# The attention's rotary score products over 128 partitions instead of 64

## The chip, the cores and the metric

The kernel runs on one core of one Trainium2 chip. The metric is the time of one execution on the device in microseconds; lower is better. The engines are called TensorE (PE, with PEld for its weight loads), VectorE (DVE), ScalarE (ACT), GpSimd (POOL) and SyncE (SP), which issues the loads.

## The reference

One residual block of a streaming encoder over 256 tokens of width 2048, all in float32. After an RMS norm, two branches run side by side, retention with 8 heads and a multi-head latent attention with 16 heads; their outputs are gated by sigmoids, added and projected, and a squared-ReLU MLP of width 8192 follows. The part that the change touches is the scores of the latent attention. A head's query and key have 128 plain elements and 64 rotary ones, and the rotary key is the same for all heads:

```python
q_nope, q_pe = q[..., :QK_NOPE], _rope(q[..., QK_NOPE:], positions)
kv = (_rmsnorm(c_kv, kv_a_norm_g) @ w_kv_b).reshape(B, S, MLA_HEADS, QK_NOPE + V_HEAD)
k_nope, v = kv[..., :QK_NOPE], kv[..., QK_NOPE:]
k_pe = _rope(k_pe.reshape(B, S, 1, QK_ROPE), positions)
qf = jnp.concatenate([q_nope, q_pe], axis=-1)
kf = jnp.concatenate([k_nope, jnp.broadcast_to(k_pe, (B, S, MLA_HEADS, QK_ROPE))], axis=-1)
my = _block_causal_attention(qf, kf, v, MLA_QK_DIM ** -0.5)
```

The mask lets a token see its own chunk of 64 tokens and all earlier ones, so the first 128 queries see only the first 128 keys.

## The kernel before

Activations lie transposed, features on the partitions. Nearly all matrix products keep float32 accuracy by splitting each operand into a rounded part (`hi`, type float32r, cast on ScalarE) and the remainder (`lo`, subtracted on VectorE), and adding three products: hi with hi, hi with lo, lo with hi. `weights` does this for a weight tile (L168 the cast, L169 the subtraction), `split` for an activation (L550, L551), `mm3` issues the three products (L583 to L585). Where a product isn't split, as for the first 128 queries' scores, it is a plain float32 product.

The stages follow each other: the first projections, retention, its output, the latent vectors (`cc`), the gates (`gm`), the attention, its output projection (`mo`), the gates' merge, the output projection (`wo`), and the MLP (`zs`, `z`, `dn`). In the stage of the gates and in the MLP the order of the instructions is written out by hand; in the attention a scheduler sets it at build time, each engine's stream being fixed from then on.

The attention goes in four groups of four heads. `mla_projections(g)` makes the queries, keys and values of a group from `cc` (products `lt`, L199 and L201; values `v`, L214 to L217). `join` adds the two halves of such a product (L540, L541). The rotary queries of a group are two tiles `pe` of 128 partitions, each with one head in partitions 0 to 63 and one in 64 to 127; `rope` turns them, and their last 128 queries are split into `pes`, which lies in the big tile `vkp`. The rotary key `kpe` is there twice, in partitions 0 to 63 and in 64 to 127, and its split `kps` lies in `vkp` too. While a group's projections run, `mla_attention` runs the group before: `mla_scores` (tile `ms`), the softmax on VectorE (L1018, L1021, L1027) and ScalarE (L1023, L1029), `mla_turn`, which transposes the probabilities (`mt`, L1036), and `mla_values` (`my`; L583 to L585 and L1052). The last group runs beside the first columns of `mo`.

In `mla_scores`, the first 128 queries take two float32 products (L1010 plain, L1011 rotary); the other 128 queries take three products of rounded parts with the plain key and three with the rotary key, each of 256 columns. The four rotary ones take the 64 partitions of their head.

Of the kernel before, what the change touches and what calls it, by code (L numbers as in the profile page):

```python
# [12 lines left out]
F32 = mybir.dt.float32  # L13
# [4 lines left out]
ALU = mybir.AluOpType  # L18

P = 128  # L20
# [85 lines left out]
def block_kernel(ctx: ExitStack, tc: tile.TileContext, A):  # L106
    nc = tc.nc
    V, SC, G, PE = nc.vector, nc.scalar, nc.gpsimd, nc.tensor
# [7 lines left out]
    def big(name, dt=F32, shape=(P, KT, S)):  # L116
        return act.tile(list(shape), dt, tag="act16", name=name)
# [31 lines left out]
    def mmps(name):  # L149
        return pmm.tile([P, 512], F32, tag="mm", name=name)  # L150

    def atps(name):
        return pat.tile([P, 512], F32, tag="at", name=name)
# [3 lines left out]
    def wtile(kind, shape):  # L157
        uid[0] += 1
        dt, bufs = (F32, 5) if kind == "raw" else (F32R, 4)
        return wp.tile(shape, dt, tag=kind, bufs=bufs, name=f"{kind}{uid[0]}")  # L160
# [33 lines left out]
    def lora_pair(src, x, spare=False):  # L194
        hi, lo = weights(src, [P, 2, LT, P])
        for i in range(2):
            ps = (atps if spare and i else mmps)(f"lt{uid[0]}{i}")
            for k in range(LT):
                PE.matmul(ps, hi[:, i, k], x.both(k), start=k == 0, stop=False)  # L199
            for k in range(LT):  # L200
                PE.matmul(ps[:, :S], lo[:, i, k], x.hi(k), start=False, stop=k == LT - 1)  # L201
            yield i, ps

    def n_unit(outs, src, x, k0, nk, start, stop):
        for kh in range(0, nk, 2):
            w = weights(src[:, kh : kh + 2], [P, 2, 512])
            first, last = start and kh == 0, stop and kh == nk - 2
            for t, out in enumerate(outs):
                n_tile(out, w, x, t, k0 + kh, 2, first, last)
# [328 lines left out]
    def join(out, ps):  # L538
        t = rope_pool.tile([P, S], F32, tag="join", bufs=2, name="join")
        SC.copy(t, ps[:, S:])  # L540
        V.tensor_tensor(out=out, in0=ps[:, :S], in1=t, op=ALU.add)  # L541
# [6 lines left out]
    def split(hi, lo, val, scale=None):  # L548
        if scale is None:
            SC.copy(hi, val)  # L550
            V.tensor_tensor(out=lo, in0=val, in1=hi.bitcast(F32), op=ALU.subtract)  # L551
        else:
            SC.activation(hi, val, AF.Copy, scale=scale)
            V.scalar_tensor_tensor(
                lo, in0=val, scalar=scale, in1=hi.bitcast(F32), op0=ALU.mult, op1=ALU.subtract
            )
# [24 lines left out]
    def mm3(out, st, mv, start=True, stop=True):  # L581
        (sh, sl), (mh, ml) = st, mv
        PE.matmul(out, sh, mh, start=start, stop=False)  # L583
        PE.matmul(out, sh, ml, start=False, stop=False)
        PE.matmul(out, sl, mh, start=False, stop=stop)  # L585
# [15 lines left out]
    for k in range(KT):  # L601
        t = lead0[:, N_VEC:] if k == 0 else wtile("raw", [P, LEAD])
# [82 lines left out]
    def rope(out, ps, cos, sin, step):  # L685
        n = ps.shape[1]
        tmp = rope_pool.tile([P, n, S], F32, tag="rope", bufs=1, name="rope")
        cos, sin = (t.rearrange("p (o n) -> p o n", o=1) for t in (cos, sin))
        for d in range(0, P, step):
            s = d + step if (d // step) % 2 == 0 else d - step  # L690
            V.tensor_tensor(
                out=tmp[d : d + step],
                in0=ps[s : s + step],
                in1=sin[s : s + step].to_broadcast([step, n, S]),
                op=ALU.mult,
            )
        V.tensor_tensor(out=out, in0=ps, in1=cos.to_broadcast([P, n, S]), op=ALU.mult)
        V.tensor_tensor(out=out, in0=out, in1=tmp, op=ALU.add)
# [210 lines left out]
    with ExitStack() as mctx:  # L909
        cc = big("cc", F32R, shape=(P, 2 * LT, 2, S))  # L910
        kpe = rope_pool.tile([P, S], F32, tag="kpe", bufs=1, name="kpe")
# [84 lines left out]
        mp = mctx.enter_context(tc.tile_pool(name="mp", bufs=1))  # L996
# [2 lines left out]
        heads, probs, outs = {}, {}, {}  # L999

        vkp = big("vkp", F32R, (P, 8, 512))
        kps = vkp[:, 4].rearrange("p (j n) -> p j n", j=2)
        split(kps[:, 0], kps[:, 1], kpe)

        def mla_scores(h):
            q0, qs, k0, ks = heads.pop(h)
            pe0, ps = heads[h // 2, "pe"]
            b = slice(64 * (h % 2), 64 * (h % 2) + 64)
            pS = atps(f"ms{h}")
            PE.matmul(pS[:, :P], q0, k0, start=True, stop=False)  # L1010
            PE.matmul(pS[:, :P], pe0[b, :P], kpe[b, :P], start=False, stop=True)  # L1011
            mm3(pS[:, P:384], (qs[:, 0], qs[:, 1]), (ks[:, 0], ks[:, 1]), stop=False)
            mm3(pS[:, P:384], (ps[b, 0], ps[b, 1]), (kps[b, 0], kps[b, 1]), start=False)
            pr = mp.tile([P, 384], F32, tag="pr", bufs=3, name=f"pr{h}")
            mx = mp.tile([P, 32], F32, tag="mx", bufs=4, name=f"mx{h}")[:, :4]
            parts = (slice(0, P), slice(P, 384))
            for j, sl in enumerate(parts):
                V.tensor_tensor_reduce(  # L1018
                    pr[:, sl], pS[:, sl], mask[:, sl], QK_SCALE, LOWEST, ALU.add, ALU.max, mx[:, j : j + 1]
                )  # L1020
            V.tensor_scalar(mx[:, :2], mx[:, :2], -1.0, None, op0=ALU.mult)  # L1021
            for j, sl in enumerate(parts):
                SC.activation(  # L1023
                    pr[:, sl], pr[:, sl], AF.Exp, bias=mx[:, j : j + 1],
                    accum_out=mx[:, 2 + j : 3 + j],
                )
            V.reciprocal(mx[:, 2:], mx[:, 2:])  # L1027
            for j, sl in enumerate(parts):
                SC.activation(pr[:, sl], pr[:, sl], AF.Copy, scale=mx[:, 2 + j : 3 + j])  # L1029
            probs[h] = pr  # L1030
# [30 lines left out]
        def mla_projections(g):  # L1061
            j0 = 2 * (g % 2)
            raw = rope_pool.tile([P, 2, S], F32, tag="val", bufs=2, name=f"raw{g}")
            for i, ps in lora_pair(A["w_qpe"][g // 2, :, j0 : j0 + 2], cq, g == 0):
                join(raw[:, i], ps)
                if i:
                    pe = mp.tile([P, 2, S], F32, tag="pe", bufs=2, name=f"pe{g}")
                    rope(pe, raw, *tabs[1], 32)
                    pes = vkp[:, 5 + g % 2].rearrange("p (i j n) -> p i j n", i=2, j=2)
                    split(pes[:, :, 0], pes[:, :, 1], pe[:, :, P:])  # L1070
                    for n in range(2):
                        heads[2 * g + n, "pe"] = pe[:, n], pes[:, n]
                yield
            for jj in range(2):
                js = slice(2 * jj, 2 * jj + 2)
                qh = []
                for i, ps in lora_pair(A["w_qn"][g, :, js], cq, g == jj == 0):
                    h = 4 * g + 2 * jj + i
                    q0 = mp.tile([P, S], F32, tag="q0", bufs=6, name=f"q0{h}")
                    qs = mp.tile([P, 2, P], F32R, tag="qs", bufs=6, name=f"qs{h}")  # L1080
                    join(q0, ps)
                    split(qs[:, 0], qs[:, 1], q0[:, P:])
                    qh.append((q0[:, :P], qs))
                    yield
                for i, ps in lora_pair(A["w_kn"][g, :, js], ckv, g == jj == 0):
                    h = 4 * g + 2 * jj + i
                    k0 = mp.tile([P, S], F32, tag="k0", bufs=6, name=f"k0{h}")
                    ks = mp.tile([P, 2, S], F32R, tag="ks", bufs=6, name=f"ks{h}")
                    join(k0, ps)
                    split(ks[:, 0], ks[:, 1], k0)  # L1090
                    heads[h] = (*qh[i], k0[:, :P], ks)
                    yield
            pss = [mmps(f"v{g}{t}") for t in range(2)]
            for kh in range(2):
                n_unit(pss, A["w_v"][g, :, 2 * kh : 2 * kh + 2], ckv, 2 * kh, 2, kh == 0, kh == 1)
                yield
            vs = vkp[:, 2 * (g % 2) : 2 * (g % 2) + 2]
            split(vs[:, 0], vs[:, 1], pss[0])
            v1 = mp.tile([P, 512], F32, tag="v1", bufs=2, name=f"v1{g}")
            SC.copy(v1, pss[1])  # L1100
            heads[g, "v"] = vs, v1
# [36 lines left out]
        for g in range(4):  # L1138
            interleave(mla_projections(g), mla_attention(g - 1) if g else iter(()))
# [431 lines left out]
```

## Time and profile before

| | |
|---|---|
| time, median of 3 runs (lowest, highest) | 1578.91 us (1578.73 to 1579.29) |
| span of the profiled execution | 1577.3 us (1.6 us under the median; its own time is not listed apart) |
| TensorE busy, its weight loads | 1565.2 us (99%), 1317.0 us (84%) |
| VectorE, ScalarE, GpSimd busy | 1313.6 us (83%), 959.0 us (61%), 38.9 us (2%) |
| granted TensorE clock, mean | 0.998 |
| the scores' products, first and last start | 598.0 and 715.7 us |

How to read the rows: a row of the timeline has the start and the duration in us, the engine, the line, the operation, and output<-inputs by the program's names. For TensorE, "128\*128 128x256" is a product over 128 rows (partitions) into 128 output columns of the array, with a moving tile of 256 columns; "64\*128" takes 64 rows. A square bracket at a row's end is the idle time ahead of it and who ended it. In the table of windows the columns are PE, PEld, DVE, ACT and POOL busy with their counts, then the granted clock, the share of the DMA engines and GB/s.

### The profile page before, as it was taken

How to read it: one execution, taken by the hardware profiler on the slowest of the kernel's cores; microseconds unless marked ns; L12 is line 12 of the kernel's file. 1: busy time of each engine (PE TensorE's matmuls, PEld its weight loads, DVE VectorE, ACT ScalarE, POOL GpSimd, SP SyncE). 2: the span in 40 equal slices, each digit the busy share in tenths (PEclk: the TensorE clock that was granted, in tenths of full speed). 3: DMA queues.
4: the chain of work that ended last, by engine and by line, in shares of the span. 5: the costliest groups of instructions: out<-in, count | busy, mean ns of one | idle time of the engine just before them, and what ended most of it. 6: DMA issues, size and time to landing. Idle time of an engine off the chain costs nothing.

```text
span 1577.3 us, 21401 instructions
## 1 busy us (share of the span) xinstructions
PE 1565.2 (99%) x7671; PEld 1317.0 (84%) x7671; DVE 1313.6 (83%) x1780; ACT 959.0 (61%) x1405; POOL 38.9 (2%) x75
## 2 busy tenths in 40 slices
PE   9999999999999999999999999999999999999997
PEld 7888888888898888888888888888888888888886
DVE  7898877899967988875667689887978899989996
ACT  6545655566545667765445566676766766666664
POOL 0000000000000000000000000010000100000000
PEclk9999999999999999999999999999999999999999
DMA  8666655466656564443565666667675977786873
GB/s 322 212 197 205 231 164 161 157 203 208 204 178 222 190 203 142 136 135 132 188 214 186 240 221 226 218 209 236 203 246 196 366 267 244 241 308 216 267 254 114
DMA packets 107626, 333.70 MB, mean 212 GB/s; under 512 B 11264, under 2 KB 12160, under 8 KB 106496
## 3 DMA queue, kind: packets, MB, share of 16 engines
q1 hardware_dynamic: 104208, 318.71, 60.5%
q0 software_dynamic: 3168, 11.54, 1.8%
q10 hardware_dynamic: 144, 2.10, 0.4%
q8 instruction: 60, 0.98, 0.3%
q14 instruction: 46, 0.38, 0.1%
HBM read 319.72 MB, written 12.58 MB: 211 GB/s over the span
## 4 chain that ended last, share of the span: by engine, by line
PE 81%; issue 0%; DVE 0%; ACT 0%; DVEq 0%; POOLq 0%; POOL 0%; ACTq 0%
PE z L176 9%; PE dn L357 7%; PE dn L359 7%; PE dn L358 7%; PE z L180 5%; PE zs L333 2%; PE zs L334 2%; PE zs L335 2%; PE lt L199 2%; PE mo L214 2%; PE mo L217 2%; PE mo L215 2%; PE wo L214 2%; PE wo L215 2%; PE wo L217 2%; PE gm L357 2%
## 5 line engine op out<-in xcount | busy, mean ns | idle before, releaser
L169 DVE TENSOR_TENSOR lo<-raw,hi 128x1024 fp32r<-128x1024 f32 (+1 forms) x148 | 173.2, 1172 | 97.2 <-ACT hi L168 97.0
L551 DVE TENSOR_TENSOR lo<-raw,hi 128x1024 fp32r<-128x1024 f32 (+3 forms) x214 | 232.3, 1102 | 22.9 <-ACT hi L550 22.5
L168 ACT CAST hi<-raw 128x1024 fp32r<-128x1024 f32 (+1 forms) x148 | 149.4, 1011 | 166.2 <-PE mo L215 46.2
L550 ACT CAST hi<-raw 128x1024 fp32r<-128x1024 f32 (+3 forms) x214 | 200.1, 954 | 55.5 <-issue 7.8
L551 DVE TENSOR_TENSOR morelo<-raw,morehi 128x1024 fp32r<-128x1024 f32 (+1 forms) x118 | 127.2, 1099 | 19.6 <-ACT morehi L550 19.1
L550 ACT CAST morehi<-raw 128x1024 fp32r<-128x1024 f32 (+1 forms) x118 | 109.1, 950 | 12.6 <-DMA raw<-w_down 3.9
L550 ACT CAST hi<-forms 128x1024 fp32r<-128x1024 f32 x70 | 73.7, 1053 | 51.7 <-DVE forms L307 28.6
L176 PE MATMUL z<-hT,morehi 128*128 128x512 f32 x408 | 101.6, 391 | 0.0
L357 PE MATMUL dn<-hi,dd 128*128 128x512 f32 x230 | 89.7, 390 | 0.0
L359 PE MATMUL dn<-hi,dd 128*128 128x512 f32 x230 | 89.6, 390 | 0.0
L358 PE MATMUL dn<-lo,dd 128*128 128x512 f32 x230 | 89.6, 389 | 0.0
L551 DVE TENSOR_TENSOR lo<-forms,hi 128x1024 fp32r<-128x1024 f32 x70 | 85.0, 1221 | 5.3 <-ACT hi L550 4.9
L176 PEld LDWEIGHTS z<-hT,morehi 128*128 128x128 f32 x408 | 74.9, 188 | 14.4
L1246 ACT COPY hs<-z 128x512 f32<-128x512 f32 x40 | 23.5, 586 | 71.1 <-PE z L180 71.1
L358 PE MATMUL dn<-morelo,dd 128*128 128x512 f32 x156 | 60.8, 390 | 0.0
L357 PE MATMUL dn<-morehi,dd 128*128 128x512 f32 x156 | 60.8, 389 | 0.0
L359 PE MATMUL dn<-morehi,dd 128*128 128x512 f32 x156 | 60.8, 389 | 0.0
L180 PEld LDWEIGHTS z<-hT,morelo 128*128 128x128 f32 x408 | 55.7, 191 | 4.0
L176 PE MATMUL z<-hT,hi 128*128 128x512 f32 x232 | 57.9, 392 | 0.0
L307 DVE TENSOR_TENSOR forms<-raw,sraw 128x1024 f32<-128x1024 f32 x46 | 56.1, 1220 | 1.0 <-DMA raw<-w_up_s 1.0
L180 PE MATMUL z<-hT,morelo 128*128 128x256 f32 x408 | 56.9, 283 | 0.0
L214 PE MATMUL mo<-hi,my 128*128 128x512 f32 x128 | 50.8, 400 | 0.0
(498 smaller groups left out, 4193.8 us busy)
## 6 DMA issues: line engine op xcount, KB each, us to landing
raw<-w_down SPq DMA_DIRECT2D x106, 512.0 KB, 6.1
raw<-w_up SPq DMA_DIRECT2D x80, 512.0 KB, 5.1
raw<-w_rv SPq DMA_DIRECT2D x32, 512.0 KB, 4.8
raw<-w_rg SPq DMA_DIRECT2D x32, 512.0 KB, 4.2
raw<-w_gret SPq DMA_DIRECT2D x32, 512.0 KB, 4.6
raw<-w_ret_o SPq DMA_DIRECT2D x32, 512.0 KB, 5.1
raw<-w_gmla SPq DMA_DIRECT2D x32, 512.0 KB, 4.6
raw<-w_mla_o SPq DMA_DIRECT2D x32, 512.0 KB, 3.7
```

What stands on the lines that cost most here:

```text
L168: SC.copy(hi, raw)
L169: V.tensor_tensor(out=lo, in0=raw, in1=hi.bitcast(F32), op=ALU.subtract)
L176: PE.matmul(out, w[0][:, k], x.both(k0 + k), start=start and k == 0, stop=False)
L180: PE.matmul(out[:, :S], w[1][:, k], x.hi(k0 + k), start=False, stop=stop and k == n - 1)
L214: PE.matmul(out, x.hi(k0 + k, ts), w[0][:, k], start=start and k == 0, stop=False)
L215: PE.matmul(out, x.lo(k0 + k, ts), w[0][:, k], start=False, stop=False)
L217: PE.matmul(out, x.hi(k0 + k, ts), w[1][:, k], start=False, stop=stop and k == nk - 1)
L357: PE.matmul(q, ah, wh, start=start, stop=False)
L358: PE.matmul(q, ah, wl, start=False, stop=False)
L359: PE.matmul(q, al, wh, start=False, stop=self.left[f] == 0)
L550: SC.copy(hi, val)
L551: V.tensor_tensor(out=lo, in0=val, in1=hi.bitcast(F32), op=ALU.subtract)
```

## The change

The four rotary products of a head no longer take 64 partitions. For the queries that are split, the stationary tile of a head holds the rounded query in the head's own 64 partitions and its remainder in the other 64. The moving tile `kcross` holds the key's remainder beside the rounded query and the rounded key beside the query's remainder, so one product gives hi with lo and lo with hi; `kround` holds the rounded key beside the rounded query, and zeros beside the remainder, and gives hi with hi. There are two of each, for heads in the lower and in the upper half, made once. For the float32 product, `kfull` holds the key in one half and zeros in the other, and the stationary tile is the whole `pe` with both heads in it. One product of 256 columns goes per head. The split of `pe` is now made in halves, the remainder written to the other half's partitions.

```diff
         vkp = big("vkp", F32R, (P, 8, 512))
-        kps = vkp[:, 4].rearrange("p (j n) -> p j n", j=2)
-        split(kps[:, 0], kps[:, 1], kpe)
+        kcross = vkp[:, 4].rearrange("p (j n) -> p j n", j=2)
+        kround = vkp[:, 7].rearrange("p (j n) -> p j n", j=2)
+        kfull = mp.tile([P, 2, P], F32, name="kfull")
+        G.memset(kfull, 0.0)
+        sides = [slice(64 * j, 64 * j + 64) for j in range(2)]
+        for j, b in enumerate(sides):
+            V.tensor_copy(kfull[b, j], kpe[b, :P])
+            SC.copy(kround[b, j], kpe[b])
+            SC.copy(kcross[b, 1 - j], kpe[b])
+        for j, b in enumerate(sides):
+            other = sides[1 - j]
+            for t in range(2):
+                SC.copy(kround[other, j, t * P : (t + 1) * P], kfull[other, j])
+            V.tensor_tensor(out=kcross[b, j], in0=kpe[b], in1=kround[b, j].bitcast(F32), op=ALU.subtract)
 
         def mla_scores(h):
             q0, qs, k0, ks = heads.pop(h)
             pe0, ps = heads[h // 2, "pe"]
-            b = slice(64 * (h % 2), 64 * (h % 2) + 64)
+            j = h % 2
             pS = atps(f"ms{h}")
             PE.matmul(pS[:, :P], q0, k0, start=True, stop=False)
-            PE.matmul(pS[:, :P], pe0[b, :P], kpe[b, :P], start=False, stop=True)
+            PE.matmul(pS[:, :P], pe0[:, :P], kfull[:, j], start=False, stop=True)
             mm3(pS[:, P:384], (qs[:, 0], qs[:, 1]), (ks[:, 0], ks[:, 1]), stop=False)
-            mm3(pS[:, P:384], (ps[b, 0], ps[b, 1]), (kps[b, 0], kps[b, 1]), start=False)
+            PE.matmul(pS[:, P:384], ps[:, j], kcross[:, j], start=False, stop=False)
+            PE.matmul(pS[:, P:384], ps[:, j], kround[:, j], start=False, stop=True)
...
                     pes = vkp[:, 5 + g % 2].rearrange("p (i j n) -> p i j n", i=2, j=2)
-                    split(pes[:, :, 0], pes[:, :, 1], pe[:, :, P:])
+                    for j, b in enumerate(sides):
+                        SC.copy(pes[b, :, j], pe[b, :, P:])
+                        V.tensor_tensor(
+                            out=pes[sides[1 - j], :, j],
+                            in0=pe[b, :, P:],
+                            in1=pes[b, :, j].bitcast(F32),
+                            op=ALU.subtract,
+                        )
```

The lines of the kernel after: L1022 is the plain float32 product of the scores and L1023 the rotary one (L1010 and L1011 before), L1025 and L1026 are the products with `kcross` and `kround`. TensorE's stream at the scores of the third head, before:

```order
L1010 MATMUL ms_5610<-k_5406,q_5368 128x128
L1011 MATMUL ms_5610<-kpe,pe_5267 128x128
L583 MATMUL ms_5610<-ks_5407,qs_5369 128x256
L584 MATMUL ms_5610<-ks_5407,qs_5369 128x256
L585 MATMUL ms_5610<-ks_5407,qs_5369 128x256
L583 MATMUL ms_5610<-vkp 128x256
L584 MATMUL ms_5610<-vkp 128x256
L585 MATMUL ms_5610<-vkp 128x256
```

and after:

```order
L1022 MATMUL ms_5624<-k_5420,q_5382 128x128
L1023 MATMUL ms_5624<-kfull,pe_5279 128x128
L583 MATMUL ms_5624<-ks_5421,qs_5383 128x256
L584 MATMUL ms_5624<-ks_5421,qs_5383 128x256
L585 MATMUL ms_5624<-ks_5421,qs_5383 128x256
L1025 MATMUL ms_5624<-vkp 128x256
L1026 MATMUL ms_5624<-vkp 128x256
```

The place in the stream is the same; of three products on `vkp` two are left. The scheduler also moves some of TensorE's transpositions, projections and value products by a few places in the later groups; from the end of the attention on, TensorE's order is the same, and the order of SyncE's loads is the same throughout.

At the start of the attention, ScalarE's stream before (`gm` are the gates' activations, `lt` the first projections, `hi` a rounded weight tile):

```order
L735 ACTIVATE gm<-gm,rx 128x512 x2
L540 COPY join<-lt_5243 128x256
L735 ACTIVATE gm<-gm,rx 128x512
L168 CAST hi_5392<-raw_5391 128x1024
L540 COPY join<-lt_5255 128x256
```

and after:

```order
L735 ACTIVATE gm<-gm,rx 128x512 x2
L540 COPY join<-lt_5255 128x256
L735 ACTIVATE gm<-gm,rx 128x512
L1014 CAST vkp<-kfull 64x128 x4
L168 CAST hi_5406<-raw_5405 128x1024
L540 COPY join<-lt_5267 128x256
```

Four casts of zeros from `kfull` into `kround` stand ahead of a weight tile's rounding. VectorE's stream at the same place, after:

```order
L169 TENSOR_TENSOR lo_5369<-raw_5367,hi_5368 128x1024
L1008 COPY kfull<-kpe 64x128 x2
L541 TENSOR_TENSOR raw_5248<-lt_5255,join 128x256
L169 TENSOR_TENSOR lo_5407<-raw_5405,hi_5406 128x1024
```

The two copies into `kfull` are new; the rest of these rows is as before. The casts and subtractions that make the other parts of `kround` and `kcross` stand earlier, in the stage of the gates, where the split of `kpe` stood.

## Prediction

> **What bounds the kernel now.** I read the page first, then the chain of waits of TensorE, then the timeline of TensorE inside the attention.
>
> ```profile
> PE 1565.2 (99%) x7671; PEld 1317.0 (84%) x7671; DVE 1313.6 (83%) x1780; ACT 959.0 (61%) x1405; POOL 38.9 (2%) x75
> PE spin L573 <- DVE cold L570: 1.2, 1, 1.2
> PE first L622 <- ACT hi L550: 1.1, 3, 0.4
> PE ms L1010 <- DVE k L541: 0.5, 1, 0.5
> PE first L622 <- DVE kk L637: 0.2, 1, 0.2
> ```
>
> The first row is the busy time of the engines; the other four are all the waits of TensorE in the whole program (total, times, longest). TensorE waits 3.0 us out of 1577.3, and only once, for 0.5 us, in the attention. So the time is the sum of what TensorE's instructions take, one after another, and a gain on TensorE counts in full as long as the others keep up. A busy TensorE says little about its pace; the pace shows in the distance from one start to the next. These rows are its timeline in the attention (start, duration, what), the first three where nothing unusual stands, the rest around one head's scores:
>
> ```profile
> 596.64 1.09 PE L199 MATMUL lt<-cc,hi 128*128 128x512 f32 x4
> 597.57 0.63 PE L201 MATMUL lt<-cc,lo 128*128 128x256 f32 x4
> 598.04 0.38 PE L1010 MATMUL ms<-k,q 128*128 128x128 f32 x2
> ...
> 641.16 0.38 PE L1010 MATMUL ms<-k,q 128*128 128x128 f32 x2
> 641.30 0.37 PE L584 MATMUL my<-pp,vkp 128*128 128x256 f32 x1
> 641.50 0.28 PE L585 MATMUL my<-pp,vkp 128*128 128x256 f32 x1
> 641.62 0.39 PE L1052 MATMUL my<-pt,v 128*128 128x128 f32 x2
> 641.94 0.49 PE L1011 MATMUL ms<-kpe,pe 64*128 64x128 f32 x2
> 642.35 0.39 PE L583 MATMUL ms<-ks,qs 128*128 128x256 f32 x1
> 642.46 0.19 PEld L584 LDWEIGHTS ms<-ks,qs 128*128 128x128 f32 x1
> 642.58 0.28 PE L584 MATMUL ms<-ks,qs 128*128 128x256 f32 x1
> 642.70 0.28 PE L585 MATMUL ms<-ks,qs 128*128 128x256 f32 x1
> 642.90 0.18 PEld L583 LDWEIGHTS ms<-vkp 64*128 64x128 f32 x1
> 642.90 0.39 PE L583 MATMUL ms<-vkp 64*128 64x256 f32 x1
> 643.13 0.28 PE L584 MATMUL ms<-vkp 64*128 64x256 f32 x1
> 643.25 0.28 PE L585 MATMUL ms<-vkp 64*128 64x256 f32 x1
> 643.46 1.19 PE L199 MATMUL lt<-cc,hi 128*128 128x512 f32 x4
> 644.48 0.28 PE L201 MATMUL lt<-cc,lo 128*128 128x256 f32 x1
> ```
>
> Undisturbed, four products of 512 columns take 597.57 - 596.64 = 0.93 us, and one of 256 columns (598.04 - 597.57) / 4 = 0.1175. A float32 product of 128 columns is two records; from 641.16 to 641.50 stand one such pair and one product of 256, so a pair is 0.34 - 0.12 = 0.22. Now the stretch from 641.62 to 644.48, 2.86 us. It holds two float32 pairs (0.44), six products of 256 (0.705) and four of 512 (0.93): 2.075 by those prices. **0.785 us is unaccounted for**, and it sits where the height changes between 128 and 64 rows ("64*128"), four times: into L1011 and out, into the three products on vkp and out. The load rows show how: inside one height the weights of L584 load from 642.46, 0.12 before their product; the 64-row weights of L583 load only from 642.90, with the product. One change of height costs 0.785 / 4 = 0.196 us.
>
> **The change part by part.**
>
> Removed: all 64-row products. In the kernel after, the scores' rotary products contract over 128 rows, so every product of the program from there on has one height. A head has two sets of 64-row products, four changes of height; there are 16 heads (the float32 product L1011 has 32 records, two to a head):
>
> ```profile
> L1011 PE MATMUL ms<-kpe,pe x32: 271/323/374, 598.4 to 714.6; 64*128 64x128 f32 x32
> 601.18 0.28 PE L584 MATMUL ms<-vkp 64*128 64x256 f32 x1
> ...
> 604.45 0.38 PE L585 MATMUL ms<-vkp 64*128 64x256 f32 x1
> ```
>
> 16 x 0.785 = 12.56, and the first head's third product on vkp stands apart from its two others (604.45 after 601.18, with full-height products between), two more changes, 0.39: 12.95. The third rotary product of each head also goes: 16 x 0.1175 = 1.88. Together **14.8 us** off TensorE. That a full-height product takes what a 64-row one does inside its height is seen in 643.13 to 643.25: 0.12 either way.
>
> The Trainium skill speaks of this from two sides. Its page "TensorE: Matmul & The Clock Gate", section "Why this matters for your kernels", says that a product of few rows takes as long as a full one and gains only by running beside another in other rows; by that the height itself costs nothing and the sum would be the 1.88 of the removed products alone. Its page "TensorEngine Tiling (Array Packing)", section "Key Properties", says that a change of tiling mode drains TensorE; by that the sum is the 14.8. Neither gives the drain a figure, and the 0.196 above is this trace's.
>
> Added at the start of the attention: on ScalarE four casts of zeros from kfull (L1014), in front of the rounding of a weight tile (L168), and on VectorE two copies into kfull (L1008), in front of a join (L541). What stands there now:
>
> ```profile
> L559 POOL MEMSET ones<- 128x128 f32 x1 | 0.2, 205 | 0.3 <-POOLq L1561 0.3
> 587.75 1.05 ACT L168 CAST hi<-raw 128x1024 fp32r<-128x1024 f32 x1 [0.30 <-ACT gm L735]
> 590.81 0.30 ACT L550 CAST qs<-q 128x128 fp32r<-128x128 f32 x1
> 588.83 1.22 DVE L169 TENSOR_TENSOR lo<-raw,hi 128x1024 fp32r<-128x1024 f32 x1 [1.55 <-ACT hi L168]
> 599.22 0.42 DVE L541 TENSOR_TENSOR k<-lt,join 128x256 f32<-128x256 f32 x1
> 599.69 0.49 PE L1010 MATMUL ms<-k,q 128*128 128x128 f32 x2 [0.54 <-DVE k L541]
> 584.00:600.00 16.00, 15.46 (x88) 13.24 (x86) 14.37 (x25) 11.64 (x22) 0.00 (x0) 1.00 0.52 164
> ```
>
> A cast of 128x128 takes 0.30, so the four take at most 1.2; overlapped by a third, some 0.8. I take 1.0: 0.3 of it fills ScalarE's idle time, 0.7 delays the cast at 587.75 and with it VectorE's subtraction at 588.83. The two copies (under 0.3 each, by the same row) fit in VectorE's 1.55 of idle before it. But VectorE has no other gap: in the last row (busy PE, PEld, DVE, ACT of that window) it is busy 14.37 of 16 us, and 1.55 is that one wait. So the join of k at 599.22 comes 0.7 later, and TensorE, which waits for it already, waits 0.7 longer; the one set's worth (0.39) that it saves before this place is waited away too. Lost: 1.1 (0.5 to 1.5). The first cast and the first copy also wait for GpSimd's memset of kfull. Behind them are queued the weight tile of L168 and the join of the first rotary query, for which TensorE's later products wait. GpSimd has no work in that window (POOL 0.00), and a memset half as large took 0.2 us at the program's start, so I put nothing for it. The casts and subtractions of the rotary key come earlier, in the stage of the gates, in 64-row pieces: three casts and one subtraction more, nothing on TensorE's path, since it does not wait in that stage.
>
> Added per group of four heads: the split of pe goes from one cast and one subtraction over 128 partitions to two of each over 64, with as many elements along each partition.
>
> ```profile
> L550 ACT CAST vkp<-pe x4: 399/403/407, 598.7 to 681.2; 128x256 fp32r<-128x256 f32 x4
> L551 DVE TENSOR_TENSOR vkp<-pe,vkp x4: 418/419/426, 601.4 to 682.4; 128x256 fp32r<-128x256 f32 x4
> 620.00:640.00 20.00, 20.00 (x116) 17.31 (x115) 17.65 (x44) 14.87 (x37) 0.00 (x0) 1.00 0.48 154
> 640.00:660.00 20.00, 20.00 (x113) 16.69 (x112) 17.04 (x45) 14.33 (x43) 0.00 (x0) 1.00 0.32 108
> 660.00:680.00 20.00, 20.00 (x117) 16.74 (x117) 17.35 (x43) 11.66 (x29) 0.00 (x0) 1.00 0.41 132
> L1011 PE MATMUL ms<-kpe,pe x14: 271/323/374, 636.6 to 677.7; 64*128 64x128 f32 x14
> ```
>
> That is 0.40 more on ScalarE and 0.42 on VectorE, four times. What hides it is VectorE's idle time, and the gain itself eats it: from 620 to 680 us VectorE is busy 17.65 + 17.04 + 17.35 = 52.04 of 60, and two groups add 0.84. Seven heads fall in there (the 14 records of the last row), and they take 7 x (0.785 + 0.1175) = 6.3 off TensorE, so the 60 become 53.7 against VectorE's 52.9. It just fits, with nothing for the moments when VectorE waits for ScalarE. I put 1.0 us of new waits there, from 0 (VectorE follows, as now) to 6.3 (the rival below).
>
> From 680 us to the end of the attention VectorE is about half busy and after it the order of TensorE and of the loads is the same, so what is gained by then is kept: all engines are only that much earlier.
>
> **Sum:** 14.8 - 1.1 - 1.0 = 12.7 us. The span of the profiled execution goes from 1577.3 to 1564.6; the median of the three runs stands 1.6 us above that span, so the time goes from 1578.91 to **1566.2 us**. The case's own range: without any loss 14.8, and with the height's price off by 0.1 us a head 1.6 more, 1562.5; with the losses 2.8 larger, 1569.
>
> **Rivals.**
>
> VectorE becomes the bound in the middle groups. For it: the 52.9 of 53.7 above. Against it: over 20 us it is never above 17.65, and TensorE does not wait for it once between 601 and the end of the attention. If nothing of the seven heads' gain got through: 14.8 - 1.1 - 6.3 = 7.4, 1571.5 us.
>
> The height is not what costs. If the 0.785 belonged to the operands (vkp and pe have just been written, or a second accumulation in the same bank) it would stay, and only the removed products count: 1.9 us, 1577.0, inside what a measurement can tell from no change (0.2%, 3.2 us). For it: the skill's sentence on small products. Against it: the products of vkp with pp at 641.30 and 641.50 read the same tile at full height, the second 0.12 before the next start.
>
> The softmax takes the drain's place, and the kernel is slower. TensorE runs in order, and a head's transposition (L1036) waits for its probabilities (ScalarE, L1029):
>
> ```profile
> 686.47 0.79 ACT L1029 ACTIVATE pr<-pr,mx 128x128 f32<-128x128 f32 x2
> 688.86 0.27 PE L1036 MATMUL mt<-con,pr 128*128 128x128 f32 x1
> ```
>
> Here the first of these two ScalarE instructions ends by 686.9, 2.0 us ahead of the transposition. Between a head's scores and its transposition stand the scores of up to three other heads, so TensorE gets there up to 2.7 us sooner. If VectorE and ScalarE could not follow at all, the worst places would wait 0.7. It decides when the waits exceed 18.0 / 16 = 1.13 us for every head (14.8 gained, and 3.2 more to be measurable); at 1.2 per head, with the start's 1.1, the time is 1578.9 - 14.8 + 19.2 + 1.1 = 1584.4. Against it: TensorE's outputs start VectorE's and ScalarE's work, so most of that slack moves along.
>
> **How the numbers follow.** The forecast has 0.70, VectorE as the bound 0.14, the height not being the cause 0.10, the softmax 0.06. Range 1562.5 to 1572.0: it holds nearly all of the first two cases. Faster by over 0.2% are the first two, with 0.84; 0.10 within 0.2%; 0.06 slower.
>
> **What would show it.** In the profile after: no row of TensorE with "64*128"; starts 0.12 apart through a head's scores, and the stretch that took 2.86 us at about 1.96; 16 products fewer; the wait of L1022 for k about 1.3 us instead of 0.5; waits of TensorE in the attention of some 2 us altogether, for VectorE. The sum is wrong if the distances stay at 0.2 with full height (the second rival), or if TensorE's waits for VectorE in the middle groups come to 5 us or more (the first), or its waits for probabilities do (the third).

## The result, and the profile after

| | before | after |
|---|---|---|
| median of 4 runs | 1578.91 us (1578.73 to 1579.29) | 1566.01 us (1565.81 to 1566.54) |
| span of the profiled execution | 1577.3 us | 1564.8 us |
| TensorE busy, products | 1565.2 us, 7671 | 1551.3 us, 7655 |

The time after is 0.9918 of the time before, with a 95% interval of 0.9904 to 0.9932: 12.9 us less. Nearly all of it comes from the attention. These rows are, for before and then for after, the last of the gates' products and the value products of all heads (count, shortest/median/longest in ns, first and last start):

```profile
L359 PE MATMUL gm<-hi,x x18: 389/390/390, 560.0 to 583.8; 128*128 128x512 f32 x18
L1052 PE MATMUL my<-pt,v x32: 270/274/276, 623.2 to 738.8; 128*128 128x128 f32 x32
```

```profile
L359 PE MATMUL gm<-hi,x x19: 389/389/389, 559.6 to 584.1; 128*128 128x512 f32 x19
L1065 PE MATMUL my<-pt,v x32: 271/274/275, 621.6 to 726.6; 128*128 128x128 f32 x32
```

From the last gates' product to the last value product it was 155.0 us and is 142.5, so 12.5 less; this stretch is called **the stage** below. What comes before it and after it takes as long as it did, within 0.3 us.

The rows of the page on busy time and on the waits of TensorE after:

```profile
PE 1551.3 (99%) x7655; PEld 1311.0 (84%) x7655; DVE 1316.0 (84%) x1787; ACT 962.6 (62%) x1416; POOL 39.3 (3%) x76
PE spin L573 <- DVE cold L570: 1.2, 1, 1.2
PE first L622 <- DVE x L554: 1.1, 2, 0.6
PE ms L1022 <- DVE k L541: 1.0, 1, 1.0
PE my L584 <- DVE pp L551: 0.7, 1, 0.7
```

TensorE is again the bound. It now waits twice in the attention, 1.7 us in all, both times for VectorE; before it was once, 0.5 us. The sixteen products that were to go are gone (7671 to 7655), and no product of the trace has 64*128 any more, where before had 80 (66 changes of height). The timeline of TensorE around one head's scores:

```profile
642.95 0.39 PE L1022 MATMUL ms<-k,q 128*128 128x128 f32 x2
643.17 0.39 PE L1023 MATMUL ms<-kfull,pe 128*128 128x128 f32 x2
643.31 0.36 PE L583 MATMUL ms<-ks,qs 128*128 128x256 f32 x1
643.52 0.28 PE L584 MATMUL ms<-ks,qs 128*128 128x256 f32 x1
643.63 0.28 PE L585 MATMUL ms<-ks,qs 128*128 128x256 f32 x1
643.75 0.28 PE L1025 MATMUL ms<-vkp 128*128 128x256 f32 x1
643.87 0.28 PE L1026 MATMUL ms<-vkp 128*128 128x256 f32 x1
643.99 0.49 PE L1049 MATMUL mt<-con,pr 128*128 128x128 f32 x3
```

Two float32 pairs and five products of 256 columns take 643.99 - 642.95 = 1.04 us; by the prediction's prices they are 2 x 0.22 + 5 x 0.1175 = 1.03. No time is left over, and the products on `vkp` start 0.12 apart on either side.

### The profile page after: what moved, and what is told of

The parts are those of the page before. It is cut to its first block, busy times and chain, and to the rows that moved or that the text cites. A ratio compares the mean times of both kernels' runs of the same rounds, so it can differ in the third digit from the quotient of the medians.

```text
span 1564.8 us, 21391 instructions
## 1 busy us (share of the span) xinstructions
PE 1551.3 (99%) x7655; PEld 1311.0 (84%) x7655; DVE 1316.0 (84%) x1787; ACT 962.6 (62%) x1416; POOL 39.3 (3%) x76
## 4 chain that ended last, share of the span: by engine, by line
PE 79%; DVE 1%; issue 1%; ACT 1%; DVEq 0%; POOLq 0%; POOL 0%; ACTq 0%
PE z L176 9%; PE dn L358 7%; PE dn L359 7%; PE dn L357 7%; PE z L180 5%; PE zs L333 2%; PE zs L334 2%; PE zs L335 2%; PE mo L214 2%; PE mo L215 2%; PE mo L217 2%; PE wo L214 2%; PE wo L215 2%; PE wo L217 2%; PE gm L357 2%; PE yr L358 2%
## 5 line engine op out<-in xcount | busy, mean ns | idle before, releaser
L169 DVE TENSOR_TENSOR lo<-raw,hi 128x1024 fp32r<-128x1024 f32 (+1 forms) x148 | 173.2, 1171 | 89.7 <-ACT hi L168 89.6
L358 PEld LDWEIGHTS dn<-lo,dd 128*128 128x128 f32 x230 | 43.2, 188 | 9.0
```

The costliest lines, as they stand in the source:

```text
L169: V.tensor_tensor(out=lo, in0=raw, in1=hi.bitcast(F32), op=ALU.subtract)
L358: PE.matmul(q, ah, wl, start=False, stop=False)
```

## The experiments

**What costs: the change of height, the 64-row product, or a product of any kind?** The first four kernels start from the kernel before.

*e1_grouped* keeps every 64-row product and changes only their order, so that a head's four stand together: 38 changes of height instead of 66.

```diff
             pS = atps(f"ms{h}")
-            PE.matmul(pS[:, :P], q0, k0, start=True, stop=False)
-            PE.matmul(pS[:, :P], pe0[b, :P], kpe[b, :P], start=False, stop=True)
             mm3(pS[:, P:384], (qs[:, 0], qs[:, 1]), (ks[:, 0], ks[:, 1]), stop=False)
             mm3(pS[:, P:384], (ps[b, 0], ps[b, 1]), (kps[b, 0], kps[b, 1]), start=False)
+            PE.matmul(pS[:, :P], pe0[b, :P], kpe[b, :P], start=True, stop=False)
+            PE.matmul(pS[:, :P], q0, k0, start=False, stop=True)
```

> The kernel before, with a head's 64-row products moved next to each other (three on vkp, then the float32 one), all of them kept: TensorE's stream has 38 changes of height instead of 66. Theory (a change of height costs 0.196 us): 28 fewer, 5.5 us, 1573.4 us. Rival (the operands or the accumulation cost, or each 64-row product does): the same products with the same operands, so 1578.9 us as before.

Measured: 1574.63 us, 0.9972 (0.9960 to 0.9983) of before's 1579.13 in the same job. The page's waits of TensorE have a new row, since the split key is now wanted first:

```profile
PE ms L584 <- DVE ks L551: 1.7, 1, 1.7
```

It stands in place of the 0.54 that before waits (here 1.70), so 1.16 us of the gain is waited away. The stage is 4.19 us shorter, and 4.19 + 1.16 = 5.35 over the 28 changes that are gone is 0.191 us for one. The same products, the same operands and the same sizes, in another order, bring the gain: that the operands, the accumulation or each 64-row product by itself cost it is ruled out.

*e2_two_of_64* keeps the 64 rows and takes one of the three products on `vkp` away.

```diff
-            mm3(pS[:, P:384], (ps[b, 0], ps[b, 1]), (kps[b, 0], kps[b, 1]), start=False)
+            PE.matmul(pS[:, P:384], ps[b, 0], kps[b, 0], start=False, stop=False)
+            PE.matmul(pS[:, P:384], ps[b, 0], kps[b, 1], start=False, stop=True)
```

> The kernel before with two of the three rotary products on vkp, still over 64 rows; the product of the query's remainder with the rounded key is left out, so the scores lack that term. 64 changes of height instead of 66. Theory: 16 products at 0.1175 us and two changes at 0.196: 2.3 us, 1576.6 us. Rival (the unaccounted 0.785 us of a head belongs to its four 64-row products, 0.196 each): 16 x (0.1175 + 0.196) = 5.0 us, 1573.9 us.

Measured: 1576.37 us, 0.9982 (0.9972 to 0.9991); the stage is 2.36 us shorter. That is the price of 16 products inside a height and the two changes of the first head (1.88 + 0.39 = 2.27). A 64-row product beside others of its height has no extra cost; its neighbours decide.

*e3_float32_only* makes the change for the float32 product alone, with the copies into `kfull`; the rounded products stay.

```diff
         split(kps[:, 0], kps[:, 1], kpe)
+        kfull = mp.tile([P, 2, P], F32, name="kfull")
+        G.memset(kfull, 0.0)
+        for j in range(2):
+            b = slice(64 * j, 64 * j + 64)
+            V.tensor_copy(kfull[b, j], kpe[b, :P])
...
-            PE.matmul(pS[:, :P], pe0[b, :P], kpe[b, :P], start=False, stop=True)
+            PE.matmul(pS[:, :P], pe0[:, :P], kfull[:, h % 2], start=False, stop=True)
```

> Only the float32 rotary product goes over 128 rows (kfull), the three on vkp stay at 64 rows: 34 changes of height. Theory: 32 fewer, 6.3 us, of which about 0.4 is waited away at the first key: 5.9 us, 1573.0 us. Rival (a cost of each 64-row product): 16 x 0.196 = 3.1 us, 1575.8 us.

Measured: 1573.21 us, 0.9959 (0.9944 to 0.9974); the stage is 5.68 us shorter with as many products as before. TensorE waits for `k` 0.4 longer:

```profile
PE ms L1015 <- DVE k L541: 0.9, 1, 0.9
```

5.68 + 0.39 = 6.07 over 32 changes is 0.190.

*e4_rounded_only* is the other half: the rounded products as after, the float32 product still on 64 rows.

```diff
...
+        kcross = vkp[:, 4].rearrange("p (j n) -> p j n", j=2)
+        kround = vkp[:, 7].rearrange("p (j n) -> p j n", j=2)
...
-            PE.matmul(pS[:, :P], pe0[b, :P], kpe[b, :P], start=False, stop=True)
+            PE.matmul(pS[:, :P], pe0[sides[j], :P], kpe[sides[j], :P], start=False, stop=True)
             mm3(pS[:, P:384], (qs[:, 0], qs[:, 1]), (ks[:, 0], ks[:, 1]), stop=False)
-            mm3(pS[:, P:384], (ps[b, 0], ps[b, 1]), (kps[b, 0], kps[b, 1]), start=False)
+            PE.matmul(pS[:, P:384], ps[:, j], kcross[:, j], start=False, stop=False)
+            PE.matmul(pS[:, P:384], ps[:, j], kround[:, j], start=False, stop=True)
...
```

> Only the rounded products are changed (two over 128 rows, with kcross and kround), the float32 rotary product stays at 64 rows: 32 changes of height and 16 products fewer. Theory: 34 x 0.196 + 1.9 = 8.5 us off TensorE, less 1.1 us of waits at the start and in the middle groups: 7.4 us, 1571.5 us. Rival (cost of each 64-row product): 48 x 0.196 + 1.9 = 11.3 less the same waits, 1568.7 us. If the start's wait comes from the four casts of zeros, TensorE waits 1 us for the first key here and about 0.5 us where only the float32 product is changed.

Measured: 1571.57 us, 0.9948 (0.9932 to 0.9965): 7.6 us less, where the theory had 7.4 and the rival 10.2. The stage is 5.68 us shorter in e3 and 7.45 in e4, 13.1 together, 0.6 over the 12.5 of the whole, whose second wait, 0.7 for `pp`, stands in neither. The waits for `k` were not as expected, about 1 us here and 0.5 in e3; they are 0.8 and 0.9:

```profile
PE ms L1021 <- DVE k L541: 0.8, 1, 0.8
```

The length of that wait is no measure of the casts, because TensorE's arrival moves too. The joins of `k` tell them apart. These are e3's, which has the two copies but no casts of zeros, and e4's, which has the casts but no copies:

```profile
599.46 0.42 DVE L541 TENSOR_TENSOR k<-lt,join 128x256 f32<-128x256 f32 x1
```

```profile
600.02 0.42 DVE L541 TENSOR_TENSOR k<-lt,join 128x256 f32<-128x256 f32 x1
```

Counted from the last gates' product (584.05 in e3, 583.99 in e4) the join ends after 15.83 us in e3, as in the kernel before, and after 16.44 in e4, as in the kernel after. So the delay comes with e4's half of the change, where the casts are, and not with the copies; in e3 TensorE only arrives 0.39 sooner. By these counts e4 loses 0.6 at the start, and 7.45 + 0.6 - 1.88 = 6.2 over its 34 changes is 0.18.

**The price by itself.** Two kernels start from the kernel after and add one product of zeros to each head, once over 128 rows and once over 64.

```diff
+        kzero = mp.tile([P, S], F32R, name="kzero")
+        SC.copy(kzero, kfull.rearrange("p j n -> p (j n)"))
...
             PE.matmul(pS[:, P:384], ps[:, j], kcross[:, j], start=False, stop=False)
+            PE.matmul(pS[:, P:384], ps[:, j], kzero, start=False, stop=False)
             PE.matmul(pS[:, P:384], ps[:, j], kround[:, j], start=False, stop=True)
```

> The kernel after with one more product of 256 columns per head, over 128 rows, with a tile of zeros: 16 products more and no change of height. Theory: 16 x 0.1175 = 1.9 us, 1567.9 us if nothing hides it; somewhat less if TensorE's waits in the middle groups shrink.

Measured for *e5_extra_128*: 1568.44 us, 0.9932 (0.9917 to 0.9947) of before's 1578.84. It is 2.4 us over the kernel after, with a stage 2.3 longer; 16 x 0.1175 is 1.9. Its waits of TensorE in the attention come to 2.07 us, 0.33 more than after, which is the rest:

```profile
PE ms L1025 <- DVE pe L698: 1.1, 1, 1.1
PE lt L199 <- DVE q L541: 0.6, 1, 0.6
...
PE lt L199 <- DVE k L541: 0.4, 1, 0.4
```

The 64-row form differs in that one line:

```diff
-            PE.matmul(pS[:, P:384], ps[:, j], kzero, start=False, stop=False)
+            PE.matmul(pS[:, P:384], ps[sides[j], j], kzero[sides[j]], start=False, stop=False)
```

> The same with the additional product of zeros over 64 rows: 16 products and 32 changes of height more than in the kernel after. Theory: 1.9 + 32 x 0.196 = 8.2 us, 1574.2 us. Rival (a cost of each 64-row product): 16 x (0.1175 + 0.196) = 5.0 us, 1571.0 us. Rival (a product's height costs nothing): 1567.9 us.

Measured for *e6_extra_64*: 1573.57 us, 0.9965 (0.9952 to 0.9978). Half as many rows are 5.1 us dearer than the whole. Its timeline of TensorE shows where:

```profile
646.09 0.29 PE L585 MATMUL ms<-ks,qs 128*128 128x256 f32 x1
646.22 0.28 PE L1027 MATMUL ms<-vkp 128*128 128x256 f32 x1
646.42 0.38 PE L1028 MATMUL ms<-kzero,vkp 64*128 64x256 f32 x1
646.74 0.38 PE L1029 MATMUL ms<-vkp 128*128 128x256 f32 x1
646.96 1.09 PE L199 MATMUL lt<-cc,hi 128*128 128x512 f32 x4
```

From 646.22 to 646.96 are three products of 256 columns, 0.35 us at 0.1175 each; it took 0.74. The two changes cost 0.39. TensorE waits less in the attention than in e5, 1.5 us and not 2.1:

```profile
PE ms L1025 <- DVE pe L698: 1.1, 1, 1.1
...
PE lt L199 <- DVE k L541: 0.4, 1, 0.4
```

The stage is 5.47 us longer than in e5 all the same: with the 0.57 us of waits, 6.04 over 32 changes, 0.189.

**Where the loss against the sum went.** *e7_zeros_early* makes the zeros of `kround` from the key in the stage of the gates, so that no cast of zeros stands in front of the weight tile at the start of the attention.

```diff
-            for t in range(2):
-                SC.copy(kround[other, j, t * P : (t + 1) * P], kfull[other, j])
+            SC.activation(kround[other, j], kpe[other], AF.Copy, scale=0.0)
```

> The kernel after with the zeros of kround made from kpe times zero on ScalarE in the stage of the gates, so that no cast stands ahead of the weight tile's rounding at the start of the attention. Theory (the four casts delay VectorE's stream and so the first key, 0.7 us): TensorE's wait for that key goes from 1.0 us to about 0.4 us and the time to 1565.4 us. Rival (VectorE's own work, the copies and the halves, sets that wait): no change, 1566.0 us.

Measured: 1565.68 us, 0.9914 (0.9898 to 0.9931); 0.3 under the kernel after, which the runs cannot tell from nothing. The wait was expected at 0.4 and stayed:

```profile
PE ms L1021 <- DVE k L541: 1.0, 1, 1.0
```

The first score starts 0.34 us earlier, counted from the last gates' product, and the join of `k` ends 0.33 earlier; both moved together, so the wait between them did not shrink. That is about half of the delay. The join still ends 0.28 later than in the kernel before, because the cast of the weight tile on ScalarE, now with no casts of zeros ahead of it, starts 4.22 us after the last gates' product and not 3.94 as before. The rival's copies on VectorE are not what holds it: e3 has them too, and its cast starts at 3.94. What does is open.

*e8_less_vector* takes most of the rotary work off VectorE, beside a kernel that is otherwise the one after.

```diff
-                    rope(pe, raw, *tabs[1], 32)
+                    V.tensor_tensor(out=pe, in0=raw, in1=tabs[1][0].rearrange("p (o n) -> p o n", o=1).to_broadcast([P, 2, S]), op=ALU.mult)
```

> The kernel after with less work for VectorE: the rotary queries are multiplied by the cosine only, the four products with the sine (L691, 0.69 us each) and the addition (L698) are left out, so the scores are not rotated properly. TensorE has the same products. Theory (what was lost of the gain are waits for VectorE: 0.4 us ahead of the first score, 1.0 us at the second key, 0.9 us at the probabilities of the second group): these go, 1563.7 us, and TensorE has no wait in the attention. Rival (the losses are TensorE's own): no change, 1566.0 us.

Measured: 1563.29 us, 0.9902 (0.9887 to 0.9917) of before's 1578.3 in its job; 2.7 us under the kernel after, or 2.1 when each is taken against before in its own job. All its waits of TensorE:

```profile
PE spin L573 <- DVE cold L570: 1.2, 1, 1.2
PE first L622 <- ACT hi L550: 0.4, 1, 0.4
PE first L622 <- DVE x L554: 0.3, 1, 0.3
```

None is in the attention. The stage takes 139.7 us, 15.3 less than before; 0.5 of that is the old wait for `k`, and 14.8 is left. So the work removed from TensorE is worth what its rows say, and what the kernel after lacks of it goes with VectorE's work.

*e9_gpsimd_half* tries to get that back with nothing left out: e7, and two of the four sine products of a group on GpSimd, which has no other work there.

```diff
-    def rope(out, ps, cos, sin, step):
+    def rope(out, ps, cos, sin, step, engines=(V, V, V, V)):
...
-            V.tensor_tensor(
+            engines[d // step].tensor_tensor(
...
-                    rope(pe, raw, *tabs[1], 32)
+                    rope(pe, raw, *tabs[1], 32, (V, V, G, G))
```

> The kernel with the zeros made early, and two of the four products with the sine of each group's rotation on GpSimd, which is idle in the attention: 1.4 us less on VectorE in each of the four bursts. Theory (VectorE's bursts set the two waits that are left): TensorE's waits of 1.0 and 0.7 us go, 1564.0 us, the fastest of all. Rival (GpSimd takes so long that the rotation comes late and TensorE waits for the rotary query): 1566 us or more.

Measured: 1567.67 us, 0.9930 (0.9913 to 0.9946): 2.0 us over e7 (the stage is 2.2 longer), where the theory had 1564.0. The groups of the sine products, first in the kernel after, then in e9:

```profile
L691 DVE TENSOR_TENSOR rope<-raw,sin x16: 679/683/689, 592.8 to 667.7; 32x512 f32<-32x512 f32 x16
```

```profile
L691 POOL TENSOR_TENSOR rope<-raw,sin x8: 1291/1636/2248, 590.3 to 668.9; 32x512 f32<-32x512 f32 x8
L691 DVE TENSOR_TENSOR rope<-raw,sin x8: 680/1248/1689, 592.7 to 668.3; 32x512 f32<-32x512 f32 x8
```

VectorE has half as many of these products, and the median of one goes from 683 to 1248 ns; its time for them falls only from 10.9 us in all to 9.6. Others are held up too, and VectorE's busy time in the stage goes from 114.8 us in e7 to 116.3, with eight products fewer. The timeline of e9 has a subtraction of a weight tile (L169), which takes about 1.22 us elsewhere, beside the first two products on GpSimd:

```profile
590.27 3.53 POOL L691 TENSOR_TENSOR rope<-raw,sin 32x512 f32<-32x512 f32 x2 [4.54 <-DVE raw L541]
590.38 2.27 DVE L169 TENSOR_TENSOR lo<-raw,hi 128x1024 fp32r<-128x1024 f32 x1
```

It takes 1.05 longer. The page "SBUF — State Buffer" of the Trainium skill, section "SBUF: two separate sides", says that VectorE and GpSimd share a pair of ports as an exclusive lock: a VectorE instruction with two inputs in SBUF and a GpSimd instruction that reads SBUF block one another for the whole of the one that came first. The trace agrees, with 0.68 against 1.25 us and 1.22 against 2.27: that subtraction starts at 590.38, GpSimd's first product ends at 591.56, and the subtraction 1.08 later, at 592.64. In e9 TensorE waits for VectorE's `pp` 1.4 us, for its `k` 1.4 and for its `ks` 0.3. The time is the rival's, but not by its path: no wait of TensorE is for the rotary query.

## Why the prediction was right, point by point

**The price of a change of height** (0.196 us, from 0.785 left over in one stretch of one head): right. e1, e3 and e6 against e5 give 0.191, 0.190 and 0.189, e4 somewhat less (0.18) and e8, where TensorE does not wait in the attention, (14.8 - 1.88) / 66 = 0.196. So 66 changes are worth 12.5 to 12.9 where the sum had 12.95. The sign by the weight loads is general: at all 66 changes of the kernel before, the load starts with its product (within 0.06 us), while inside a height it starts 0.11 us ahead in the median. The "Key Properties" of the Trainium skill's page "TensorEngine Tiling (Array Packing)", by which a change of mode drains TensorE, agree with 0.19 us a change; that a drain is what takes the time is not shown beyond that. What the page "TensorE: Matmul & The Clock Gate" says in "Why this matters for your kernels", that a product of few rows takes as long as a full one, holds inside a height (e2) and not across one (e6).

**The removed products** (1.88): right; 16 fewer, and the starts in a head's scores are 0.12 apart. The stretch forecast at 1.96 comes to 1.97, put together from the 1.04 above and the 0.93 of four products of 512 columns; it does not stand in one piece in the timeline after.

**The start of the attention** (1.1 lost): about right in size. In the kernel after, ScalarE and VectorE stand there like this:

```profile
587.04 0.72 ACT L735 ACTIVATE gm<-gm,rx 128x512 f32<-128x512 f32 x1
587.78 1.00 ACT L1014 CAST vkp<-kfull 64x128 fp32r<-64x128 f32 x4
588.69 1.04 ACT L168 CAST hi<-raw 128x1024 fp32r<-128x1024 f32 x1
589.76 1.23 DVE L169 TENSOR_TENSOR lo<-raw,hi 128x1024 fp32r<-128x1024 f32 x1 [1.67 <-ACT hi L168]
600.15 0.42 DVE L541 TENSOR_TENSOR k<-lt,join 128x256 f32<-128x256 f32 x1
600.62 0.49 PE L1022 MATMUL ms<-k,q 128*128 128x128 f32 x2 [1.00 <-DVE k L541]
```

The four casts run right in front of the weight tile's and move it from 587.75 to 588.69, VectorE's subtraction from 588.83 to 589.76, and the join of `k` from 599.22 to 600.15. Counted from the last gates' product, which is itself 0.3 later, these are 0.6 (0.7 forecast). The product L1022 that waits for `k` starts 0.6 later on the same count (before at 599.69), and the first set's 0.39, saved ahead of it, is waited away as forecast: 1.0 lost. The wait itself shows 1.0 where about 1.3 was put, because TensorE also reached the first score 0.36 later than before. The delay comes with the half that has the zero casts and not with the copies (e4, e3); but taking the casts away (e7) won back only half of it, and the other half is open.

**The cover in the middle groups** (1.0 lost, from 0 to 6.3): right, and it was nearly used up. The windows after (busy PE, PEld, DVE, ACT, POOL):

```profile
620.00:640.00 20.00, 19.27 (x119) 17.01 (x118) 18.88 (x49) 15.77 (x42) 0.00 (x0) 1.00 0.42 138
640.00:660.00 20.00, 20.00 (x119) 17.43 (x118) 18.55 (x49) 17.75 (x49) 0.00 (x0) 1.00 0.39 133
660.00:680.00 20.00, 20.00 (x131) 18.04 (x129) 19.19 (x48) 14.96 (x37) 0.00 (x0) 1.00 0.39 132
```

VectorE goes from 52.04 to 18.88 + 18.55 + 19.19 = 56.6 of 60, and TensorE waits for it once, 0.7 us at the first head's values, which run beside the second group's projections:

```profile
620.23 0.28 PE L583 MATMUL my<-pp,vkp 128*128 128x256 f32 x1
621.24 0.39 PE L584 MATMUL my<-pp,vkp 128*128 128x256 f32 x1 [0.73 <-DVE pp L551]
```

Between these starts are 1.01 us instead of 0.12, 0.9 lost.

**The sum**: 14.8 - 2.1 = 12.7 forecast, 12.5 measured in the spans and in the stage. Of the 2.3 lost, 1.0 and 0.9 are the two places above; 0.4 is spread over gaps that no row of the waits shows; in e8 it is not lost. The medians differ by 12.9, because the median after stands 1.2 us above its profiled span and that before 1.6; the execution profiled after took 1566.54 us, the longest of the four. That the median came within 0.2 us of the forecast is therefore in part luck: the losses at the two places came 0.2 lower than put, and the 0.4 was in no term.

**The rivals.** VectorE as the bound: its condition was close, but TensorE's waits in the middle groups are 0.7 us and not 5; e8, whose gain is 2.1 to 2.8 by the times and the stage, bounds what this work of VectorE costs in all. The height not being the cause: refuted by e1, which changes the order alone, and by e6 against e5, which changes the rows of one product alone. The softmax: no transposition waits for its probabilities, though TensorE gets there sooner; the 0.7 us for `pp`, the remainder of the transposed probabilities, is the one wait behind the softmax, for VectorE and far from the 18 us that this rival needed.

## What to carry to other kernels

Where TensorE is the bound, look at the distance between starts rather than at busy time, and at the rows where the number of partitions contracted over changes: here a lone 64-row product among 128-row ones costs 0.12 us for itself and 0.39 for going in and out. If it can't be filled to the full height (with zeros, or better, with a remainder that needs its own product anyway), group the small ones; e1 got 4.5 us of the 12.9 by order alone. Price the gain against the engine that feeds TensorE: each microsecond saved takes one from its idle time, and after this change 3.4 of 60 us were left in the middle groups.

## What the runs showed of the hardware that was not expected

Work given to an idle GpSimd slowed VectorE more than it relieved it: in e9 a VectorE product of 32x512 went from 0.68 to 1.25 us in the median, and on GpSimd the same took 1.3 to 2.2. Forecast here, but not what its work suggests: a product of half the rows was dearer than one of all rows by 5.1 us over 16 of them, 0.32 each, although it has half the work, because it stood alone among full ones.
